# RWKV-7 inverse per pair of heads, diagonal state, and own tiles for the modulation weights

## The chip, the cores and the metric

The kernel runs on one core of a Trainium2 chip. The metric is the device time of one execution in microseconds (us), the median of the runs. TensorE (PE) multiplies matrices; a matmul loads its stationary operand (PEld in the profile) and streams the other. VectorE (DVE), ScalarE (ACT) and GpSimd (POOL) do the elementwise work, and all transfers here are issued on the queue of SyncE (SP).

## The reference

Two blocks run one after the other, all in fp32. The first has 512 tokens of width 1024, projects them with one matrix and feeds four mixers with four heads of 64 each; the second has two layers on 512 tokens and 256 of context. What matters here is the first block, and of the second the modulation that is computed from the conditioning vector alone.

```python
def rwkv7_time_mix(p, ...):            # one of the four mixers
    ...
    def step(state, inp):
        r_t, w_t, k_t, v_t, kk_t, a_t = inp
        sa = jnp.einsum('bhij,bhj->bhi', state, -kk_t)
        state = (state * w_t[:, :, None, :]
                 + sa[..., None] * (kk_t * a_t)[:, :, None, :]
                 + v_t[..., None] * k_t[:, :, None, :])
        return state, jnp.einsum('bhij,bhj->bhi', state, r_t)

def first_block(x, ...):
    h = rms_norm(x, norm_g[l])
    p = h @ w_in[l]
    (fq, fk, fv, fg, ff, sq, sk, sv, sg, rw, rg, lx, lg) = split_columns(p)
    y_fox = forgetting_attention(...)  # causal softmax with log forget gates
    y_sb = stick_breaking_attention(...)
    y_rw = rwkv7_time_mix(rw, ...)
    y_lru = rg_lru(lx, ...)
    y = jnp.concatenate([y_fox * silu(fg), y_sb * silu(sg), y_rw * silu(rg), y_lru * silu(lg)], -1)
    x = x + y @ w_out[l]
    ...
```

## The kernel before

**Layout.** Activations lie with the feature in the partitions: `x` and `y` are eight tiles of 128 features by 512 tokens. Matrices are multiplied at more than half precision by splitting: ScalarE writes the high part of a weight tile (`wh`, L149), VectorE the rest (`wl`, L150), and the same is done for the activations (`hH`, `hL`). Each product is then three matmuls, L178, L179 and L182 in the feature-major projection `proj_a`, or L202 to L204 in `proj_b`. A weight tile (`wtile`) is 128x1024 fp32, 512 KB, from a pool with three raw buffers `wr` and two each of `wh` and `wl`. It serves 24 matmuls of 512 columns.

**The order.** The program is written mixer by mixer in the order of `B_ORDER` (L41): `rw` RWKV, `sq` and `st` projection and core of stick-breaking attention, `fq` projection of fox (the forgetting attention), `lr` RG-LRU, `g4 g2 g6` three gate projections, `ad` the modulation of the first layer, `fo` the core of fox, `g0` its gate. A list scheduler then places each engine's instructions; a step that is written earlier has the higher priority, and a step whose inputs or buffers are late is passed by later ones. Each engine takes its list strictly in order. Buffers of the elementwise tiles come from lanes, with a count each (`B_LANES`); PSUM has three banks for `rw`, two for `at` (the attentions), one for `ad` and two for the projections.

**RWKV.** The 512 tokens are cut into four blocks of 128 (`b`), and the four heads into two pairs, each pair in the 128 partitions. `rwkv_gram` (L736) builds the products of the decayed operands inside each block (L762 multiplies one of them with v). `rwkv_inverse` (L765) inverts a unit triangular matrix for each block and head, by six levels of doubling: at each level GpSimd masks (L796), TensorE makes three products with 64x64 pieces (`prod`, L781), VectorE subtracts (L804, L805). `rwkv_free` (L821) multiplies the inverse with what needs no state (L828, L834). `rwkv_block` (L839) then walks the four blocks: u from the state (L848), the new state (L855, L856), the output (L866, L867, L869) and its copy by ScalarE (L870). The state of a pair is one 128x128 tile, of which a mask keeps the two diagonal quarters.

**Fox.** For each of four query tiles and four heads: scores (L534, with forget terms at L536 and L538), maximum (L540), exponential (L542), normalisation (L543, L544), transposes on TensorE (L397). After each second head follows the product with v (L521). The widths of the four query tiles are 128, 256, 384 and 512.

**The modulation.** `ada` (L954) runs over 12 groups. Of each it reads 2 MB of `wada` as four tiles of 512 KB in `wr` buffers, 48 in all, and multiplies 32 columns of the conditioning by it: 32 matmuls per group at L968, each two passes in the trace (384 matmuls, 768 passes). Then the row is copied, transposed (L397) and added to the bias in `mod` (L976).

**What follows.** `out_split` (L1169) projects `y` (L1185 to L1187). The residual additions are L439 and L444. The gate of a mixer is applied in `gates` (L481): ScalarE's activation (L486), VectorE's product (L488).

## Time and profile before

| | |
|---|---|
| median of 3 runs | 2241.99 us (2240.73 to 2243.96) |
| the profiled execution | 2235.85 us, span of its records 2234.1 us |
| mean granted clock of TensorE | 0.961 of 2.4 GHz |
| instructions | 31919 |
| busy: PE, PEld, DVE, ACT, POOL | 93%, 75%, 58%, 44%, 9% |
| chain of waits that ended last | PE 73%, DVE 13%, ACT 5%, DMA 5% |
| moved by DMA | 221.94 MB, mean 99 GB/s |

The busy share is of the whole span. The first phase, up to the first matmul of `out_split` at 440.6 us, is a fifth of it; the rest is that projection and the second block. PEclk in a window is the share of full clock that was granted, a mean over the stretch. A line of the waits gives an instruction group and what ended its waiting; a line of a group gives its shapes (partitions x elements), the count, busy time, the mean of one in ns, and the idle time of its engine ahead of it.

### The profile page before, as it was taken

Reading aid. Unit: us, or ns where it says so; the run is one execution under the profiler, and the core shown is the slowest. Engines: PE = TensorE matmul, PEld = TensorE weight load, DVE = VectorE, ACT = ScalarE, POOL = GpSimd, SP = SyncE. Lnnn points to the kernel's source line nnn. Section 1 sums busy time; section 2 is a strip of 40 time slices with the busy share of each in tenths; the row PEclk is TensorE's granted clock in tenths of the full one; section 3 lists DMA queues with packets and bytes.
Section 4 is the critical chain, followed back from the end, with each engine's and each line's share of the span. In section 5 each row is a group of like instructions: output and inputs, shape, how many; then the busy total and the mean of one; then the engine's idle time right before and its main releaser. Section 6 shows DMA issues by size and latency. Waiting matters only on the chain.

```text
span 2234.1 us, 31919 instructions
## 1 busy us (share of the span) xinstructions
PE 2078.4 (93%) x12676; PEld 1683.9 (75%) x12676; DVE 1293.1 (58%) x2275; ACT 990.2 (44%) x1874; POOL 193.6 (9%) x150
## 2 busy tenths in 40 slices
PE   6998997787999989989999999989988998999999
PEld 5876784577885847778888888879957756787877
DVE  5554523277655566576987344677656656554554
ACT  5533622254556764453132232455656554332432
POOL 0012100004000100230000000053000001000000
PEclk9998999898999989999999999999998999999999
DMA  4210137543110213432675212244212222232232
GB/s 154 76 57 2 42 108 244 191 132 105 48 53 6 81 38 116 162 114 90 203 236 164 73 51 81 89 148 139 72 50 70 69 77 71 90 101 92 82 112 85
DMA packets 86853, 221.94 MB, mean 99 GB/s; under 512 B 12976, under 2 KB 23984, under 8 KB 86576
## 3 DMA queue, kind: packets, MB, share of 16 engines
q1 hardware_dynamic: 86704, 219.90, 30.3%
q8 instruction: 100, 1.64, 0.3%
q14 instruction: 49, 0.40, 0.1%
HBM read 212.53 MB, written 7.34 MB: 98 GB/s over the span
## 4 chain that ended last, share of the span: by engine, by line
PE 73%; DVE 13%; ACT 5%; DMA 5%; issue 2%; POOL 0%; SPq 0%; DVEq 0%; ACTq 0%
PE ps L178 14%; PE ps L179 14%; PE ps L182 14%; PE ps L203 3%; PE ps L204 3%; PE ps L202 3%; DVE wl L150 2%; DMA wr<-in_wadaT 2%; PE ps L1448 2%; PE ps L1185 2%; PE ps L1186 2%; PE ps L1187 2%; DMA wr<-in_wada 2%; PE ps L521 1%; PE ps L397 1%
## 5 line engine op out<-in xcount | busy, mean ns | idle before, releaser
L178 PE MATMUL ps<-hH,wh 128*128 128x512 f32 (+1 forms) x1424 | 511.1, 364 | 20.2 <-ACT wh L149 13.0
L179 PE MATMUL ps<-hL,wh 128*128 128x512 f32 (+1 forms) x1424 | 501.9, 362 | 1.6 <-DVE hL L150 0.9
L149 ACT CAST wh<-wr 128x1024 fp32r<-128x1024 f32 (+4 forms) x302 | 284.1, 943 | 458.6 <-PE ps L179 378.5
L150 DVE TENSOR_TENSOR wl<-wr,wh 128x1024 fp32r<-128x1024 f32 (+4 forms) x266 | 288.6, 1087 | 253.4 <-ACT wh L149 244.9
L182 PE MATMUL ps<-hH,wl 128*128 128x512 f32 (+1 forms) x1248 | 432.4, 371 | 1.8 <-DVE wl L150 1.6
L178 PEld LDWEIGHTS ps<-hH,wh 128*128 128x128 f32 x1424 | 272.5, 192 | 73.6 <-ACT wh L149 14.8
L179 PEld LDWEIGHTS ps<-hL,wh 128*128 128x128 f32 x1424 | 272.4, 191 | 44.5 <-issue 1.8
L182 PEld LDWEIGHTS ps<-hH,wl 128*128 128x128 f32 x1248 | 223.5, 190 | 37.9 <-DVE wl L150 4.5
L203 PE MATMUL ps<-wl,hH 128*128 128x256 f32 x704 | 204.2, 291 | 12.6 <-DVE wl L150 12.5
L202 PE MATMUL ps<-wh,hH 128*128 128x256 f32 x704 | 204.4, 292 | 0.3 <-ACT wh L149 0.3
L204 PE MATMUL ps<-wh,hL 128*128 128x256 f32 x704 | 202.2, 290 | 0.0
L178 PE MATMUL ps<-uH,wh 128*128 128x512 f32 (+1 forms) x528 | 188.1, 362 | 7.0 <-ACT uH L149 4.1
L179 PE MATMUL ps<-uL,wh 128*128 128x512 f32 (+1 forms) x528 | 181.9, 358 | 0.2 <-DVE uL L150 0.2
L182 PE MATMUL ps<-uH,wl 128*128 128x512 f32 (+1 forms) x488 | 155.4, 365 | 2.5 <-DVE wl L150 2.4
L203 PEld LDWEIGHTS ps<-wl,hH 128*128 128x128 f32 x704 | 138.5, 197 | 16.2 <-DVE wl L150 14.6
L202 PEld LDWEIGHTS ps<-wh,hH 128*128 128x128 f32 x704 | 137.7, 196 | 4.0 <-issue 2.6
L204 PEld LDWEIGHTS ps<-wh,hL 128*128 128x128 f32 x704 | 137.8, 197 | 0.8 <-issue 0.3
L150 POOL TENSOR_TENSOR wl<-wr,wh 128x1024 fp32r<-128x1024 f32 (+1 forms) x36 | 84.1, 2343 | 603.8 <-ACT wh L149 584.4
L1691 DVE SCALAR_TENSOR_TENSOR xy<-ps,mod,xy 128x512 f32<-128x512 f32 (+1 forms) x96 | 60.8, 659 | 127.6 <-PE ps L182 124.5
L178 PEld LDWEIGHTS ps<-uH,wh 128*128 128x128 f32 x528 | 99.6, 189 | 34.2 <-ACT wh L149 8.4
L145 ACT COPY t<-ps 128x512 f32<-128x512 f32 (+4 forms) x131 | 64.3, 496 | 121.0 <-PE ps L397 70.6
L179 PEld LDWEIGHTS ps<-uL,wh 128*128 128x128 f32 x528 | 100.0, 189 | 15.9 <-DVE uL L150 0.7
(359 smaller groups left out, 3272.5 us busy)
## 6 DMA issues: line engine op xcount, KB each, us to landing
wr<-in_up SPq DMA_DIRECT2D x110, 512.0 KB, 3.6
wr<-in_wada SPq DMA_DIRECT2D x48, 512.0 KB, 4.4
wr<-in_wadaT SPq DMA_DIRECT2D x48, 512.0 KB, 4.3
wr<-in_win2b SPq DMA_DIRECT2D x36, 512.0 KB, 3.6
wr<-in_win SPq DMA_DIRECT2D x30, 512.0 KB, 3.6
wr<-in_dn SPq DMA_DIRECT2D x40, 320.0 KB, 2.9
wr<-in_dn SPq DMA_DIRECT2D x32, 384.0 KB, 3.2
wr<-in_wout SPq DMA_DIRECT2D x12, 512.0 KB, 3.7
```

Source lines behind the costliest of these rows:

```text
L145: self.nc.any.tensor_copy(out, in_)
L149: self.nc.scalar.copy(hi, src)
L150: (eng or self.nc.vector).tensor_tensor(lo, src, hi.bitcast(F32), ALU.subtract)
L178: nc.tensor.matmul(acc[s], wh, fh(k), start=(q == 0), stop=False)
L179: nc.tensor.matmul(acc[s], wh, fl(k), start=False, stop=False)
L182: nc.tensor.matmul(acc[s], wl, fh(k), start=False, stop=(q == nk - 1))
L202: nc.tensor.matmul(bank[:, i], fh(k), wh, start=start, stop=False)
L203: nc.tensor.matmul(bank[:, i], fh(k), wl, start=False, stop=False)
L204: nc.tensor.matmul(bank[:, i], fl(k), wh, start=False, stop=stop)
L1185: nc.tensor.matmul(acc, wh, yH[:, k], start=(q == 0), stop=False)
L1186: nc.tensor.matmul(acc, wh, yL[:, k], start=False, stop=False)
L1691: nc.vector.scalar_tensor_tensor(s.x[:, d, :], acc, self.mcol(5, d, s), s.x[:, d, :], ALU.mult, ALU.add)
```

## The change

Two parts of the program are written anew. The rest is the same text.

**RWKV.** The two heads of a pair share their tiles in the inverse, so that a level is one set of eight 64-column pieces instead of two of four. The products of the keys with v, inside the block for the output (`yk`) and for the state (`kv`), are made in `rwkv_gram` for all blocks at once, and `kv` is multiplied by the decay `fac` there. The state tiles are cleared once by GpSimd, and a block writes only the two 64x64 diagonal quarters; its output is VectorE's addition of `yk` instead of ScalarE's copy.

**The modulation.** `ada` reads tiles of 128x512, 256 KB, one for each of the eight row blocks of a group, 96 in all, into four buffers of their own (`wa`). The RWKV lane has 20 buffers instead of 29.

```diff
-B_LANES = dict(rw=29, at=4, qkv=5)
+B_LANES = dict(rw=20, at=4, qkv=5, wa=4)
...
-            zp = self.ps([P, 4, 64], "rw")
-            for b in range(4):
-                nc.tensor.matmul(zp[:, b], ga[:, b], tk("v", h, b), start=True, stop=True)
-            nc.scalar.copy(z[:, :, h], zp)
+            zp = self.ps([P, 2, 4, 64], "rw")
+            for e, m in enumerate((ga, gk)):
+                for b in range(4):
+                    nc.tensor.matmul(zp[:, e, b], m[:, b], tk("v", h, b), start=True, stop=True)
+            nc.scalar.copy(z[:, :, h], zp[:, 0])
+            nc.scalar.copy(yk[:, :, h], zp[:, 1])
+        kv = self.work.tile([P, 3, 64], F32, name=self.nm("kv"), tag="kv", bufs=2)
+        kp = self.ps([P, 3, 64], "rw")
+        for b in range(3):
+            for h in range(2):
+                nc.tensor.matmul(kp[h * 64 : h * 64 + 64, b], tk("ka", h, b), tk("v", h, b), start=True, stop=True)
+        nc.vector.tensor_tensor(kv, kp, d["fac"][:, 0:3]..., ALU.mult)
...
         for l in range(6):
-            for gb, up, cuh, clh, gd in heads:
-                an, xx = (t[:, i] for t in (two(),) for i in range(2))
-                nc.gpsimd.tensor_tensor(an, gd, c4(lmask[:, l : l + 1]), ALU.mult)
+            for d in pairs:
+                cu, cl = d["cu"], d["cl"]
+                an = t8()
+                nc.gpsimd.tensor_tensor(an, d["gd"], c8(lmask[:, l : l + 1]), ALU.mult)
...
-                tx = prod(cuh, lambda q, b: xx[q, b])
-                px = prod(xx, lambda q, b: cuh[q, b])
-                nc.vector.tensor_tensor(clh, clh, tx, ALU.subtract)
-                nc.vector.tensor_tensor(cuh, cuh, px, ALU.subtract)
+                tx = prod(cu, lambda q, u: xx[q, u])
+                px = prod(xx, lambda q, u: cu[q, u])
+                nc.vector.tensor_tensor(cl, cl, tx, ALU.subtract)
+                nc.vector.tensor_tensor(cu, cu, px, ALU.subtract)
...
+        d["sn"] = [self.work.tile([P, P], F32, name=self.nm("sn"), tag="sn", bufs=6) for _ in range(3)]
+        for sn in d["sn"]:
+            nc.gpsimd.memset(sn, 0.0)
...
-            sp = self.ps([P, P], "rw")
-            nc.tensor.matmul(sp, tok["be"][:, s], u, start=True, stop=False)
-            nc.tensor.matmul(sp, tok["ka"][:, s], tok["v"][:, s], start=False, stop=True)
...
-                nc.vector.tensor_tensor(sn, st, sp, ALU.add)
-                nc.vector.scalar_tensor_tensor(sn, sn, fac[:, b : b + 1], self.hsum, ALU.mult, ALU.mult)
+            base, f = kv[:, b], fac[:, b : b + 1]
+            if st is not None:
+                base = work.tile([P, 64], F32, name=self.nm("sb"), tag="sb", bufs=2)
+                for q in halves:
+                    nc.vector.scalar_tensor_tensor(base[q], st[q, q], f[q], kv[q, b], ALU.mult, ALU.add)
+            sp = self.ps([P, 64], "rw")
+            for h, q in enumerate(halves):
+                nc.tensor.matmul(sp[q], tk("be", h, b), u[:, h], start=True, stop=True)
+            sn = d["sn"][b]
+            for q in halves:
+                nc.vector.scalar_tensor_tensor(sn[q, q], sp[q], f[q], base[q], ALU.mult, ALU.add)
...
-            nc.tensor.matmul(yp[:, h], d["gk"][h][:, b], tk("v", h, b), start=(h == 0), stop=False)
-            nc.tensor.matmul(yp[:, h], d["gb"][h][:, b, 1, :], u[:, h], start=False, stop=(h == 1 and st is None))
+            nc.tensor.matmul(yp[:, h], d["gb"][:, 4 * h + b, 1, :], u[:, h], start=(h == 0),
+                             stop=(h == 1 and st is None))
...
-        nc.scalar.copy(y4[:, b], yp)
+        nc.vector.tensor_tensor(y4[:, b], yp, d["yk"][:, b], ALU.add)
...
-            for k0 in range(0, KT, 2):
-                w = self.wtile("wr")
-                self.dma(w.rearrange("p (k c) -> p k c", k=2), a["wada"][g, k0 : k0 + 2].rearrange("k p c -> p k c"))
-                for i in range(2):
-                    k = k0 + i
-                    for j in range(4):
-                        nc.tensor.matmul(acc[32 * j : 32 * j + 32, :], self.sc[:, k, :],
-                                         w[:, i * 512 + j * P : i * 512 + (j + 1) * P],
-                                         start=(k == 0), stop=(k == KT - 1))
+            for k in range(KT):
+                w = self.work.tile([P, 512], F32, name=self.nm("wa"), tag="wa", bufs=self.lanes["wa"])
+                self.dma(w, a["wada"][g, k])
+                for j in range(4):
+                    nc.tensor.matmul(acc[32 * j : 32 * j + 32, :], self.sc[:, k, :], w[:, j * P : (j + 1) * P],
+                                     start=(k == 0), stop=(k == KT - 1))
```

**What moves.** The scheduler places the instructions of the first phase in another order. In the new program the matmul of `ada` is at L979, and those of `rwkv_free` are at L836 and L842, of `rwkv_block` at L872 (state) and L879 (output), of `out_split` at L1195 to L1197.

SP's queue before, where the tiles of `wada` (`wr` from `in_wada`) follow the last tiles of the first block's projection weights (`in_win1`):

```order
L138 DMA wr509_2722<-in_win1 128x1024
L138 DMA wr512_2728<-in_win1 128x1024
L138 DMA wr519_2790<-in_win1 128x1024
L138 DMA wr522_2796<-in_win1 128x1024
L138 DMA wr532_2862<-in_wada 128x2x512
L138 DMA wr533_2872<-in_wada 128x2x512
L138 DMA wr534_2882<-in_wada 128x2x512
L138 DMA t2736_3838<-in_xT 128x512
```

After, in the first half of the block's projections:

```order
L138 DMA wr63_378<-in_win1 128x1024
L138 DMA wa513_2880<-in_wada 128x512
L138 DMA wa514_2886<-in_wada 128x512
L138 DMA wa515_2892<-in_wada 128x512
L138 DMA wr70_440<-in_win1 128x1024
L138 DMA wa516_2898<-in_wada 128x512
L138 DMA wr73_446<-in_win1 128x1024
L138 DMA wa520_2910<-in_wada 128x512
L138 DMA wr302_1712<-in_win1 128x1024
L138 DMA wa521_2916<-in_wada 128x512
L138 DMA wr305_1718<-in_win1 128x1024
```

The tiles of `wada` now stand between those of the projections, from the block's start on.

TensorE before, from the last product of fox (L521) over the last groups of `ada` (L968, row transposes L397) to the gate projection `g0` (L178, with `hH`), behind which the output projection L1185 comes:

```order
L521 MATMUL ps719_3726<-t2718_3724,t2451_2303 64x128
L397 MATMUL ps600_3318<-ident_131,row599_3316 128x128
L968 MATMUL ps601_3321<-wr602_3322,sc_96 32x128 x8
L968 MATMUL ps601_3321<-wr603_3332,sc_96 32x128 x8
...
L397 MATMUL ps607_3364<-ident_131,row606_3362 128x128
L968 MATMUL ps608_3367<-wr609_3368,sc_96 32x128 x8
...
L397 MATMUL ps614_3410<-ident_131,row613_3408 128x128
L178 MATMUL ps726_3748<-hH13_148,wh721_3737 128x512
```

After, within fox's seventh pair of heads, and at the end of the phase:

```order
L397 MATMUL ps705_3666<-ident_131,t2704_3662 128x128 x3
L521 MATMUL ps707_3672<-t2700_3653,t2416_2242 64x128
L979 MATMUL ps618_3395<-wa625_3432,sc_96 32x128 x4
L979 MATMUL ps618_3395<-wa626_3438,sc_96 32x128 x4
L521 MATMUL ps707_3672<-t2706_3670,t2416_2242 64x128
...
L521 MATMUL ps733_3762<-t2732_3760,t2417_2243 64x128
L1195 MATMUL ps749_3861<-hH744_3845,wh747_3856 128x512
```

The last `ada` matmuls stand inside fox's chain, the gate projection is ahead of them, and the output projection follows fox directly.

TensorE before, the first steps of RWKV's blocks (L855, L856 state; L866, L867 output), which stand behind the last gate projection:

```order
L855 MATMUL ps284_1604<-t2275_1567,t2100_575 128x128
L856 MATMUL ps284_1604<-t2104_589,t2102_582 128x128
L968 MATMUL ps531_2861<-wr532_2862,sc_96 32x128 x5
L968 MATMUL ps531_2861<-wr533_2872,sc_96 32x128 x3
L866 MATMUL ps286_1609<-t2104_589,t2132_676 128x64
L867 MATMUL ps286_1609<-t2275_1567,gb130_674 128x64
```

After, the same steps (L872 state, L879 output) behind the last of `rwkv_free` (L842):

```order
L842 MATMUL ps246_1534<-up175_832,t2123_651 64x128 x8
L872 MATMUL ps252_1552<-t2237_1503,t2100_575 64x64 x2
L178 MATMUL ps457_2546<-hH13_148,wh447_2493 128x512
L179 MATMUL ps457_2546<-hL14_149,wh447_2493 128x512
L182 MATMUL ps457_2546<-hH13_148,wl448_2494 128x512
...
L178 MATMUL ps457_2546<-hH13_148,wh447_2493 128x512
L879 MATMUL ps253_1557<-t2237_1503,gb130_674 128x64 x2
L179 MATMUL ps457_2546<-hL14_149,wh447_2493 128x512
```

They stand between the matmuls of a gate projection (L178, L179, L182).

## Rows read from the trace of the kernel before

**Rows 1.** The page, part 1: busy us, share of span, instructions.

```profile
PE 2078.4 (93%) x12676; PEld 1683.9 (75%) x12676; DVE 1293.1 (58%) x2275; ACT 990.2 (44%) x1874; POOL 193.6 (9%) x150
```

**Rows 2.** Windows: stretch, length, busy (PE, PEld, DVE, ACT, POOL), clock, DMA share, GB/s.

```profile
22.50:150.00 127.50, 124.18 (x581) 97.71 (x581) 69.11 (x105) 65.49 (x99) 13.86 (x14) 1.00 0.22 73
150.00:205.00 55.00, 48.08 (x419) 34.47 (x419) 23.91 (x45) 13.70 (x36) 10.36 (x17) 0.84 0.03 11
205.00:309.30 104.30, 101.30 (x1197) 79.91 (x1193) 45.12 (x81) 51.24 (x88) 13.89 (x22) 0.98 0.14 47
...
341.50:410.00 68.50, 53.45 (x651) 31.68 (x650) 20.05 (x60) 18.40 (x52) 2.66 (x1) 0.88 0.74 244
410.00:425.50 15.50, 7.43 (x130) 4.22 (x131) 0.62 (x5) 1.58 (x3) 0.00 (x0) 0.71 0.83 273
```

**Rows 3.** Waits of PE, 326 to 425 us: total us, times, longest us.

```profile
PE ps L968 <- DMA wr<-in_wada: 13.4, 16, 2.0
PE ps L397 <- ACT row L145: 3.0, 6, 0.7
PE ps L968 <- DVE mod L976: 2.2, 5, 0.7
```

**Rows 4.** Timeline of PE, g0 and the projection: start, us, work, idle before.

```profile
431.94 0.39 PE L182 MATMUL ps<-hH,wl 128*128 128x512 f32 x1
...
438.75 0.39 PE L182 MATMUL ps<-hH,wl 128*128 128x512 f32 x1
...
440.62 0.73 PE L1185 MATMUL ps<-hH,wh 128*128 128x512 f32 x2 [1.48 <-ACT hH L149]
```

**Rows 5.** Timeline of PE in the heads of fox.

```profile
343.08 0.70 PE L534 MATMUL ps<-t,xy 64*128 64x256 f32 x2
...
346.45 0.70 PE L534 MATMUL ps<-t,xy 64*128 64x256 f32 x2
...
369.31 0.91 PE L534 MATMUL ps<-t,xy 64*128 64x384 f32 x2
...
373.15 0.91 PE L534 MATMUL ps<-t,xy 64*128 64x384 f32 x2
...
400.61 1.12 PE L534 MATMUL ps<-t,xy 64*128 64x512 f32 x2
...
404.64 0.63 PE L397 MATMUL ps<-ident,t 128*128 128x128 f32 x4 [0.67 <-DVE t L544]
...
407.51 1.97 PE L521 MATMUL ps<-t,t 128*64 128x128 f32 x14
```

**Rows 6.** Timeline of PE: ada, gram, free.

```profile
329.59 1.50 PE L968 MATMUL ps<-wr,sc 128*32 128x128 f32 x42
...
173.01 1.06 PE L762 MATMUL ps<-t,t 128*128 128x64 f32 x8
...
310.32 2.00 PE L828 MATMUL ps<-t,t 128*128 128x64 f32 x16
...
317.19 0.49 PE L855 MATMUL ps<-t,t 128*128 128x128 f32 x2
```

**Rows 7.** Groups by line, 0 to 700 us: busy, mean ns, idle before.

```profile
L804 DVE TENSOR_TENSOR t<-t,ps 128x256 f32<-128x256 f32 x20 | 8.3, 413 | 15.8 <-PE ps L781 15.7
L488 DVE TENSOR_TENSOR xy<-xy,t 128x512 f32<-128x512 f32 x8 | 5.5, 688 | 11.6 <-ACT t L486 11.6
L796 POOL TENSOR_TENSOR t<-t,masks 128x256 f32<-128x256 f32 x24 | 19.0, 799 | 71.8 <-PE ps L781 65.7 <-ACT t L565 2.9 <-PE ps L762 2.5
```

**Rows 8.** DMA issues: KB each, median us from issue to landing.

```profile
wr<-in_win SPq DMA_DIRECT2D x30, 512.0 KB, 3.6
t<-in_lruw SPq DMA_DIRECT2D x1, 256.0 KB, 2.5
```

**Rows 9.** Waits of PE, 438 to 503 us; VectorE's timeline there.

```profile
PE ps L1185 <- DVE xy L439: 6.2, 2, 3.7
440.81 4.90 DVE L150 TENSOR_TENSOR hL<-xy,hH 128x512 fp32r<-128x512 f32 x8
```

More of the change, by code (lines that the diff above doesn't have):

```diff
@@ L771, in rwkv_inverse @@
-        c4 = lambda x: x.to_broadcast([P, 4, 64])
-        t4 = lambda t: t.rearrange("p (b t) -> p b t", b=4)
-        two = lambda: self.t2().rearrange("p (h b t) -> p h b t", h=2, b=4)
-        idc = c4(lmask[:, 6:7])
+        lo, hi = halves = (slice(0, 64), slice(64, 128))
+        c8 = lambda x: x.to_broadcast([P, 8, 64])
+        t8 = lambda: self.t2().rearrange("p (u t) -> p u t", u=8)
+        idc = c8(lmask[:, 6:7])
         def prod(lhs, rhs):
-            out = self.ps([P, 4, 64], "rw")
-            for b in range(4):
+            out = self.ps([P, 8, 64], "rw")
+            for u in range(8):
@@ L780, in prod @@
                 for q in halves:
-                    nc.tensor.matmul(out[q, b], lhs[q, b], rhs(q, b), start=True, stop=True)
+                    nc.tensor.matmul(out[q, u], lhs[q, u], rhs(q, u), start=True, stop=True)
             return out
-        heads = []
         for d in pairs:
-            cu, cl, gd = two(), two(), two()
-            d["up"] = [t4(self.t2()) for _ in range(2)]
-            for h in range(2):
-                nc.gpsimd.memset(d["up"][h][64:128, :, 0:64], 0.0)
-                for q in halves:
-                    nc.gpsimd.tensor_copy(gd[q, h], d["gb"][h][q, :, 0, q])
-                heads.append((d["gb"][h], d["up"][h], cu[:, h], cl[:, h], gd[:, h]))
+            d["cu"], d["cl"], d["gd"] = t8(), t8(), t8()
@@ L803, in rwkv_inverse @@
-                px = prod(xx, lambda q, b: cuh[q, b])
-                nc.vector.tensor_tensor(clh, clh, tx, ALU.subtract)
-                nc.vector.tensor_tensor(cuh, cuh, px, ALU.subtract)
-        lo, hi = halves
-        for gb, up, cuh, clh, _ in heads:
-            for q in halves:
-                nc.gpsimd.tensor_copy(up[q, :, q], cuh[q])
-            xp = self.ps([P, 4, 64], "rw")
-            for b in range(4):
-                nc.tensor.matmul(xp[hi, b], gb[lo, b, 0, hi], clh[lo, b], start=True, stop=True)
-            xx = two()[:, 0]
+                xx = t8()
@@ new lines, in rwkv_inverse @@
+                self.copy(xx, prod(an, lambda q, u: cl[q, u]))
+                tx = prod(cu, lambda q, u: xx[q, u])
+                px = prod(xx, lambda q, u: cu[q, u])
+                nc.vector.tensor_tensor(cl, cl, tx, ALU.subtract)
+                nc.vector.tensor_tensor(cu, cu, px, ALU.subtract)
+        for d in pairs:
+            cu, cl, gb, up = d["cu"], d["cl"], d["gb"], d["up"]
+            for q in halves:
+                nc.gpsimd.tensor_copy(up[q, :, q], cu[q])
+            xp = self.ps([P, 8, 64], "rw")
+            for u in range(8):
+                nc.tensor.matmul(xp[hi, u], gb[lo, u, 0, hi], cl[lo, u], start=True, stop=True)
+            xx = t8()
@@ L815, in rwkv_inverse @@
             self.copy(xx[hi], xp[hi])
-            px = self.ps([P, 4, 64], "rw")
-            for b in range(4):
-                nc.tensor.matmul(px[lo, b], xx[hi, b], cuh[hi, b], start=True, stop=True)
+            px = self.ps([P, 8, 64], "rw")
+            for u in range(8):
+                nc.tensor.matmul(px[lo, u], xx[hi, u], cu[hi, u], start=True, stop=True)
             nc.scalar.activation(up[lo, :, hi], px[lo], AF.Copy, scale=-1.0)
@@ L827, in rwkv_free @@
             for b in range(4):
-                nc.tensor.matmul(up0[:, b, h], up[h][:, b], z[:, b, h], start=True, stop=True)
+                nc.tensor.matmul(up0[:, b, h], up[:, 4 * h + b], z[:, b, h], start=True, stop=True)
         d["u0"] = self.t2().rearrange("p (b h i) -> p b h i", b=4, h=2)
```

34 lines of the change are left out of this document (17 added, 17 removed).

## The prediction

> **What bounds the kernel now.** I read the page first. TensorE (PE) is busy for 93% of the span [rows 1], and the instruction orders of the two programs differ, names apart, only up to the first output projection of the first block (the loop of out_split, L1185). So what has to be forecast is one number: how much earlier that projection starts. The first phase, where all edits lie, is then cut by stage [rows 2]. From 22.5 to 150 us and again from 205 to 309 us PE hardly idles: projections run back to back. The weak stretches are 150 to 205 us (6.9 us idle, granted clock 0.84, that is a mixture of the two levels 1.2 and 2.4 GHz), 341 to 410 us (15 us idle, 0.88) and 410 to 425 us (8 us idle, 0.71). In the last two DMA moves 244 to 273 GB/s, nearly all of it the modulation weights of ada.
>
> Why PE idles there is in its waits: between 326 and 425 us it stood 13.4 us for wr tiles of in_wada, and 5.2 us more for the row copies and the mod additions that end a group of ada [rows 3]. After 410 us there is nothing but ada, tile after tile at the pace of the transfers, and the gate projection g0 and the output projection (start 440.62 us) queue behind it on PE, g0 at 0.227 us a pass (30 passes from 431.94 to 438.75 us) [rows 4]. The attention of fox lies in the same stretch. It is a chain of its own: scores, softmax on VectorE and ScalarE, transposes, product. PE takes the heads one after the other, and each ada tile that has not landed pushes the next link back [rows 5]. So this stage is bound by two things at once, the bytes of ada and the chain of fox, since in_wada shares the three wr buffers with the projections' weights and stands behind all of them on SP's queue.
>
> **The change, part by part.**
>
> Ada. Its 96 tiles of 256 KB get four buffers of their own. The order shows what comes of that: 224 of the 384 ada matmuls now stand ahead of fox's second query tile, in 32 places (before, only three stand ahead of the end of the last gate projection), the first four tiles ahead of the first projection; 160 (40 tiles) stay in the tail. PE's price for a pass is 0.0357 us (42 passes in 1.50 us [rows 6]), and each matmul is two passes. Of the 224, 16 fall before the first projection, where PE waits for the norm anyway, and 73 stand among the steps of stick, between 175 and 212 us, where PE had 6.9 us of idle [rows 2]; these are free. The other 135 cost 135 x 2 x 0.0357 = 9.6 us of a PE that is full. The 73 fill 5.2 us of the idle in stick; if that cover were gone it would be 5.2 us more. The 1.7 us of idle that are left there I count as a gain, since ada's passes fill them with work that need not be done later.
>
> RWKV. In the inverse, pairs of products of 4x64 columns become one of 8x64: the same 480 matmuls, so PE gains nothing. VectorE: 40 subtractions of 0.41 us become 20 of about 0.69 us (the price of a 512-wide one), so 16.5 us become 13.8 (the other group of 20, L805, has the same mean); POOL: 24 of 0.80 us (19.0 us) become 12 of twice the width, at most the same 19.0 us, at least half [rows 7]. Both engines are half idle there and PE hardly waits for them, so I cost this at nothing; the cover is the stick and projection work that stands between the levels. Bounds: no gain below 0, and at most the 2.7 us of VectorE. The kappa products (12 matmuls for the state, 16 for y) move out of the steps into the gram. At 0.12 us a pass with a 128-row weight (8 passes in 1.06 us [rows 6]) they cost 28 x 2 x 0.12 = 6.7 us of full PE. The triangular products L828 and L834, 7.0 us from 310.3 to 317.2 us, and the block steps stood in the tail and now stand between the projections of the gates. The new steps hold 40 matmuls: 40 x 2 x 0.12 = 9.6 us. The chain of a step loses one VectorE addition and gains split halves; with projections between the links nobody waits for it. The six memsets of the states on POOL and the eight additions that replace ScalarE's copies of y run on engines with room. So RWKV adds 6.7 + 7.0 + 9.6 = 23.3 us ahead of the tail and takes its steps out of it.
>
> Start of the tail. The last gate projection ended at 309.3 us. Now: 309.3 + 9.6 + 23.3 - 1.7 = 340.5 us.
>
> The tail. Six pairs of heads remain (two of each width 256, 384, 512), and g0. Score to score within a pair takes 3.4 us at 256 columns and 3.8 at 384 (with ada between), and at 512 4.0 us to the transposes and 0.6 for these, 4.6 in all [rows 5]. For copy and product I add 1.2, 1.7 and 2.3 us (the 14 passes of the last took 1.97 us). So a pair is 2 x 3.4 + 1.2 = 8.0, 2 x 3.8 + 1.7 = 9.3, and 2 x 4.6 + 2.3 = 11.5 us; all six 57.6 us. g0, 48 matmuls at 0.227 us (10.9 us), stands between the first two heads, in which PE idles for an estimated half of the 3.4 us, 1.7 us each: 7.5 us more. The first pair thus ends at 340.5 + 8.0 + 7.5 = 356.0 us. The next three pairs (8.0 + 9.3 + 9.3 = 26.6 us) carry 32 of the tail's 40 tiles. Four are in the buffers; 28 tiles, 7.3 MB, at the 244 GB/s of this stage [rows 2] need 30.1 us. So the transfers are late by 3.5 us there. I add 1.4 us for the latency of a refill (256 KB landed in 2.5 us [rows 8], at 244 GB/s a tile comes every 1.1), and 2.4 us for the ends of the five groups (5.2 us in 11 waits, 0.47 us each [rows 3]): 7.3 us. The last two pairs (23.0 us) have no ada. End: 356.0 + 26.6 + 7.3 + 23.0 = 412.9 us, instead of 440.6: 27.7 us.
>
> Behind it. Rows 2, 3, 6, 7 of y are split for the output projection during fox now (the order has six of the eight subtractions early), where before all eight, 4.9 us of VectorE, stood at 440.8 us and made PE wait 6.2 us for L439, which was queued behind them [rows 9]. I take half of that wait, 3 us; the bounds are 0 and 6.2.
>
> SP's queue carries 48 issues more and is in order: a wa issue whose buffer is still held blocks the wr issues behind it. In the places where they alternate, wr is fetched one projection (24 passes, 5.4 us) ahead, so up to some 3 us of blocking cost nothing. The transfer itself: 512 KB landed in 3.6 us and 256 KB in 2.5 us [rows 8], so half the size costs 70% of the time, and 48 transfers more carry 48 x 1.4 = 67 us of latency in all. With four in flight and an empty queue that is hidden up to 309 us; in the tail it is in the 1.4 us. The Trainium skill (DMA: Bandwidth & Descriptors, section Bandwidth) speaks against this edit: transfers should be batched to 1 MiB or more, and its section on the anatomy of one DMA gives each a fixed cost of about 2.0 us. By that alone, with nothing hidden, the 48 added transfers would be 96 us, an estimate from the page, and the kernel slower; the rows have a smaller step, and whether it shows is the second rival below.
>
> Sum: 27.7 + 3.0 = 30.7 us off the profiled execution of 2235.85 us (span 2234.1), so 2205. The median of the runs is 2241.99, 6 us above that execution, and 30.7 us off it is 2211 us.
>
> **The rivals.** Larger gain: the waits in the tail vanish (7.3 us), the blocks fill idle PE and the tail starts 6 us sooner, and at a full granted clock the six pairs lose 5 us; with the 31 us that is 49 us: 2193 us. For it: the tail's stretches have 0.88 and 0.71 today [rows 2]. Against it: PE stays half idle there, as now.
>
> The transfers bind. With 1 MB in flight instead of 1.5 MB the rate falls to two thirds of 244, to 163 GB/s, and the 28 tiles take 45 us instead of 30: 15 us less gain, 2226 us. For it: the tail empties all four buffers within one head, so a refill cannot start early. Against it: the landing time falls with the size. This is where the rule of the Trainium skill (DMA: Bandwidth & Descriptors, section Bandwidth) would show.
>
> Given back: the output projection starts early but finds its weights late, as wout's tiles stand among ada's last tiles on SP. Losing 12 us there makes 2223 us. Against it: the first five are ahead of the last ada tile.
>
> Slower: the 32 places ahead of the tail stop a full PE, each until its tile lands, since PE is in order and SP's queue holds wa behind wr. A wait for in_wada was 0.84 us on average and 2.0 us at most [rows 3]. At 0.96 us each the gain is gone; at 1.3 us the sum is 42 us and the time 2253 us. Against it: up to 309 us DMA is busy for 22% or less [rows 2], and a tile has one projection's time to land.
>
> That the change doesn't do what it says can be excluded for the placement, which the order shows.
>
> **How the numbers follow.** Forecast 0.57 (its own range 2200 to 2219), larger gain 0.15, the transfers bind 0.13, given back 0.06, slower 0.05, and 0.04 for a sum near zero from several of these. The forecast and the first three rivals are all faster: 0.91. About 0.2% (4.5 us) is what a measurement can tell from no change; same 0.04, slower 0.05. The range 2190 to 2230 holds the forecast, most of the larger gain and both small gains, some 0.85; it reaches to the bounds of the hL term and of the transfer rate.
>
> **What would show it.** The first ada matmul before 22 us; the output projection's first matmul near 413 us; PE idle for in_wada's tiles in the tail a few us instead of 13.4, and under 5 us in all ahead of it; no stretch with ada alone; the inverse's products at the same sum of PE time. I am wrong if the last gate projection ends much later than 340 us (waits in the full stretch), if heads in the tail are further apart than 5 us (transfers), or if the time from the output projection's start to the end grows.

## The result, and the profile after

The changed kernel takes 2217.43 us (median of 4 runs, 2213.03 to 2220.95), the kernel before in the same comparison 2242.70 us. The ratio is 0.9887, interval 0.9868 to 0.9907: 25.3 us less. The forecast was 2211 us and faster; the range 2190 to 2230 us holds the time, and the gain is 5.4 us smaller than the 30.7 forecast.

In the profiled execution (2217.67 us, span 2215.9) TensorE is as full as it was [rows 1]:

```profile
PE 2075.2 (94%) x12700; PEld 1678.3 (76%) x12700; DVE 1296.4 (59%) x2267; ACT 991.5 (45%) x1864; POOL 185.5 (8%) x134
```

The windows of the changed kernel, columns as in [rows 2] and with cuts at its own landmarks, show where it went. The last gate projection but g0 ends at 334.1 us, the first of the remaining pairs of fox's heads at 352.3, the fourth at 389.5, and the output projection starts at 419.1:

```profile
22.50:150.00 127.50, 123.31 (x701) 93.52 (x701) 65.98 (x108) 63.82 (x99) 10.38 (x8) 1.00 0.36 120
150.00:205.00 55.00, 53.27 (x470) 39.21 (x470) 22.89 (x43) 15.37 (x41) 9.47 (x10) 1.00 0.19 58
205.00:309.30 104.30, 103.17 (x1555) 83.90 (x1555) 53.64 (x103) 51.28 (x87) 9.37 (x10) 1.00 0.28 87
309.30:334.10 24.80, 24.80 (x114) 19.84 (x112) 14.08 (x26) 13.06 (x19) 0.00 (x0) 1.00 0.24 73
334.10:352.30 18.20, 18.20 (x168) 13.63 (x167) 6.23 (x14) 7.56 (x16) 0.00 (x0) 1.00 0.59 195
352.30:389.50 37.20, 31.31 (x300) 16.93 (x299) 9.58 (x27) 9.52 (x28) 0.00 (x0) 0.72 0.61 205
389.50:419.10 29.60, 19.07 (x67) 9.54 (x66) 6.17 (x14) 7.95 (x17) 2.65 (x1) 0.58 0.00 1
```

From 150 to 205 us the idle 6.9 us are 1.7 now, and the granted clock is 1.00 instead of 0.84. From 205 us to the end of the gates PE is full. Then the clock falls: 0.72 over the next three pairs, 0.58 over the last two, the lower level (0.5 is 1.2 GHz) for most of it, with DMA idle. What PE waits for there (its waits from 326 to 425 us, in total us, times, longest us) is another thing than in [rows 3]:

```profile
PE ps L397 <- DVE t L544: 11.9, 7, 3.2
PE ps L979 <- DMA wa<-in_wada: 2.1, 6, 0.6
PE ps L397 <- ACT row L145: 1.8, 3, 0.9
```

The 13.4 us for in_wada are 2.1, and fox's own chain, VectorE's normalisation at L544, has come up as the wait, with 11.9 us.

The timeline of PE (start, duration, work, idle before): the end of the last gate projection, the first scores of three pairs, the scores, transposes and product of the last, and the output projection:

```profile
333.83 0.39 PE L182 MATMUL ps<-hH,wl 128*128 128x512 f32 x1
...
352.31 0.70 PE L534 MATMUL ps<-t,xy 64*128 64x256 f32 x2
...
389.51 1.12 PE L534 MATMUL ps<-t,xy 64*128 64x512 f32 x2
...
402.92 2.07 PE L534 MATMUL ps<-t,xy 64*128 64x512 f32 x2
...
415.35 1.09 PE L397 MATMUL ps<-ident,t 128*128 128x128 f32 x4 [3.15 <-DVE t L544]
...
416.37 2.77 PE L521 MATMUL ps<-t,t 128*64 128x128 f32 x16
...
419.08 0.80 PE L1195 MATMUL ps<-hH,wh 128*128 128x512 f32 x1
```

Two scores of 512 columns took 2.07 us here; in [rows 5] the same took 1.12. The projection starts 21.5 us sooner than in [rows 4]. From there to the end of the span it is 1796.8 us instead of 1793.5, so 18.2 us of the span are gained. That is 7.1 us less than the medians give: the profiled execution of the kernel before (2235.85 us) lies 6.9 us under the median of its runs, that of the changed kernel at its median. Where these 7 us lie, two profiles do not show.

### The profile page after: what moved, and what is told of

It is laid out like the page before. It is cut to its first block, busy times and chain, and to the rows that moved or that the text cites. A ratio compares the mean times of both kernels' runs of the same rounds, so it can differ in the third digit from the quotient of the medians.

```text
span 2215.9 us, 31987 instructions
## 1 busy us (share of the span) xinstructions
PE 2075.2 (94%) x12700; PEld 1678.3 (76%) x12700; DVE 1296.4 (59%) x2267; ACT 991.5 (45%) x1864; POOL 185.5 (8%) x134
## 4 chain that ended last, share of the span: by engine, by line
PE 75%; DVE 12%; ACT 6%; DMA 4%; issue 2%; POOL 0%; SPq 0%; POOLq 0%; DVEq 0%; ACTq 0%
PE ps L178 15%; PE ps L179 14%; PE ps L182 14%; PE ps L203 3%; PE ps L204 3%; PE ps L202 3%; DVE wl L150 2%; PE ps L1458 2%; DMA wr<-in_wadaT 2%; PE ps L1195 2%; PE ps L1196 2%; PE ps L1197 2%; PE ps L397 2%; PE ps L1449 1%; PE ps L790 1%
## 5 line engine op out<-in xcount | busy, mean ns | idle before, releaser
L178 PE MATMUL ps<-hH,wh 128*128 128x512 f32 (+1 forms) x1424 | 509.3, 363 | 16.5 <-ACT wh L149 13.0
L179 PE MATMUL ps<-hL,wh 128*128 128x512 f32 (+1 forms) x1424 | 499.4, 361 | 1.5 <-DVE hL L150 0.8
L182 PE MATMUL ps<-hH,wl 128*128 128x512 f32 (+1 forms) x1248 | 431.2, 370 | 4.7 <-DVE wl L150 4.6
L150 DVE TENSOR_TENSOR wl<-wr,wh 128x1024 fp32r<-128x1024 f32 (+4 forms) x266 | 289.3, 1090 | 247.2 <-ACT wh L149 237.0
L178 PEld LDWEIGHTS ps<-hH,wh 128*128 128x128 f32 x1424 | 270.3, 190 | 70.6 <-ACT wh L149 14.7
L179 PEld LDWEIGHTS ps<-hL,wh 128*128 128x128 f32 x1424 | 270.3, 190 | 44.3 <-issue 2.8
L182 PEld LDWEIGHTS ps<-hH,wl 128*128 128x128 f32 x1248 | 222.8, 189 | 41.3 <-DVE wl L150 7.6
L203 PE MATMUL ps<-wl,hH 128*128 128x256 f32 x704 | 204.8, 292 | 12.7 <-DVE wl L150 12.6
L178 PE MATMUL ps<-uH,wh 128*128 128x512 f32 (+1 forms) x528 | 188.3, 363 | 6.5 <-ACT uH L149 3.7
L179 PE MATMUL ps<-uL,wh 128*128 128x512 f32 (+1 forms) x528 | 182.2, 358 | 0.2 <-DVE uL L150 0.2
L182 PE MATMUL ps<-uH,wl 128*128 128x512 f32 (+1 forms) x488 | 155.4, 365 | 1.8 <-DVE wl L150 1.8
L178 PEld LDWEIGHTS ps<-uH,wh 128*128 128x128 f32 x528 | 99.7, 189 | 33.9 <-ACT wh L149 8.4
L179 PEld LDWEIGHTS ps<-uL,wh 128*128 128x128 f32 x528 | 100.1, 190 | 15.8 <-DVE uL L150 0.7
```

Source lines behind the costliest of these rows:

```text
L150: (eng or self.nc.vector).tensor_tensor(lo, src, hi.bitcast(F32), ALU.subtract)
L178: nc.tensor.matmul(acc[s], wh, fh(k), start=(q == 0), stop=False)
L179: nc.tensor.matmul(acc[s], wh, fl(k), start=False, stop=False)
L182: nc.tensor.matmul(acc[s], wl, fh(k), start=False, stop=(q == nk - 1))
L203: nc.tensor.matmul(bank[:, i], fh(k), wl, start=False, stop=False)
```

## The experiments

Each ratio is to runs of the kernel before on the same chip, with its 95% interval. "Start" is the output projection's first matmul in the profiled execution, "rest" the span behind it.

| kernel | median us | ratio to before | start us | rest us |
|---|---|---|---|---|
| before | 2242.70 | | 440.6 | 1793.5 |
| changed | 2217.43 | 0.9887 (0.9868 to 0.9907) | 419.1 | 1796.8 |
| e1 ada's own tiles alone | 2213.56 | 0.9877 (0.9840 to 0.9914) | 414.0 | 1799.8 |
| e2 RWKV alone | 2237.98 | 0.9993 (0.9971 to 1.0015) | 443.9 | 1799.7 |
| e3 changed, 512 KB tiles | 2210.46 | 0.9880 (0.9840 to 0.9920) | 426.2 | 1779.4 |
| e4 changed, extra work | 2202.48 | 0.9841 (0.9803 to 0.9879) | 414.9 | 1787.2 |
| e5 changed once more | 2216.27 | 0.9909 (0.9885 to 0.9932) | 415.4 | 1796.6 |
| e6 changed, g0 late | 2203.13 | 0.9852 (0.9825 to 0.9879) | 426.3 | 1782.5 |
| e7 changed, fox in RWKV's banks | 2176.97 | 0.9735 (0.9703 to 0.9767) | 395.8 | 1784.0 |
| e8 e7 and g0 late | 2192.00 | 0.9812 (0.9781 to 0.9842) | 402.7 | 1785.4 |
| e9 e7, six wa buffers | 2180.27 | 0.9730 (0.9690 to 0.9770) | 396.1 | 1781.2 |
| e10 before, fox in RWKV's banks | 2231.42 | 0.9955 (0.9934 to 0.9975) | 449.9 | 1779.7 |
| e11 e1, fox in RWKV's banks | 2240.12 | 0.9993 (0.9971 to 1.0014) | 452.6 | 1780.6 |

The table has to be read by its last two columns. The rest of the program computes the same everywhere, yet it takes from 1779 to 1800 us. The scheduler plans the whole program with simulated times, so an edit in the first phase changes its choices later on: behind the start, the traces have 31 of TensorE's some 9290 matmuls in another place in the changed kernel than before, in e1 to e4 and e6 to e11 476 to 1191. When these lists are laid side by side, the difference lies in one stretch: between 300 and 480 us behind the start e3, e4, e6, e7, e9, e10 and e11 gain 12 to 17 us on the kernel before, the changed kernel (both profiles) and e2 at most 2, e8 4 and e1 7. Which choice there is worth it was not tried. Start and rest are of one execution each, and the executions of one kernel lie up to 18 us apart (e2: 2229.96 to 2248.13 us, with 2245.39 the profiled one). So a theory on the first phase is judged by the start, and a median only together with the rest.

**Once more the same (e5).**

> The changed kernel itself once more, beside the next ones. The first runs of one and the same kernel lay 8 us apart, and the stretch from the output projection's start to the end, the same instructions in the same order, took between 1779 and 1800 us. Expected: projection start within 3 us of 419.1, the rest between 1779 and 1800, and a median of 2210 to 2220 us.

The start, from the timeline:

```profile
415.36 0.80 PE L1195 MATMUL ps<-hH,wh 128*128 128x512 f32 x1
```

It lies 3.7 us before that of the first profile, a little outside the expected 3; the rest is the same to 0.2 us. A start is thus known to about 4 us, and the gain in the start is 21.5 to 25.3 us.

**Ada's tiles alone (e1) and RWKV alone (e2).** e1 is the kernel before with the new reads of ada:

```diff
-B_LANES = dict(rw=29, at=4, qkv=5)
+B_LANES = dict(rw=25, at=4, qkv=5, wa=4)
...
-            for k0 in range(0, KT, 2):
-                w = self.wtile("wr")
...
+            for k in range(KT):
+                w = self.work.tile([P, 512], F32, name=self.nm("wa"), tag="wa", bufs=self.lanes["wa"])
+                self.dma(w, a["wada"][g, k])
```

> The kernel before with ada's own tiles alone (four of 256 KB); RWKV is the old code, with 25 lane buffers instead of 29. Theory 1, the gain is the bytes of ada that leave the tail: most of the 25 us is here, 2219 to 2226 us, ada's passes lie in the stick stretch and its granted clock is near 1.00 instead of 0.84. Rival, the gain is RWKV's shorter program: 2236 to 2245 us.

The windows of e1, stick stretch, columns as above:

```profile
150.00:205.00 55.00, 52.22 (x446) 36.08 (x449) 22.60 (x46) 13.87 (x37) 6.91 (x13) 1.00 0.30 96
```

and the projection's first matmul (timeline):

```profile
414.01 0.50 PE L1182 MATMUL ps<-hH,wh 128*128 128x512 f32 x1 [0.82 <-ACT t L486]
```

e2 is the changed kernel with that edit undone.

> The changed RWKV with ada as before, in the 512 KB wr tiles. Theory 1: the tail is still bound by ada's transfers, so 2232 to 2242 us, the output projection starts no earlier than 432 us, PE waits over 10 us for in_wada in the tail and the clock of the stick stretch stays near 0.84. Rival, the RWKV change alone shortens the phase: 2217 to 2226 us.

Its waits of PE from 300 to 445 us:

```profile
PE ps L981 <- DMA wr<-in_wada: 18.9, 17, 2.8
```

the stick stretch in the windows, and the projection's first matmul:

```profile
150.00:205.00 55.00, 49.87 (x492) 38.30 (x492) 22.07 (x37) 12.93 (x33) 10.61 (x11) 0.91 0.03 11
```

```profile
443.94 0.73 PE L1198 MATMUL ps<-hH,wh 128*128 128x512 f32 x2 [1.49 <-ACT hH L149]
```

The start comes forward by 26.6 us in e1, whose median is even better than expected, and goes back by 3.3 in e2, less than the 4 us to which a start is known. Ada's own tiles are the whole gain of the changed kernel, and RWKV's new form by itself gains nothing: PE still waits for in_wada at the end, 18.9 us in e2. The stick stretch tells the same of the clock: 1.00 with ada's passes in it, 0.91 without them in e2, 0.84 in [rows 2]. In e1 RWKV's steps, in the old form, still stand in the tail, between the heads of fox. That e2's clock lies between the two while it has no ada there, since the kappa products (L763, L770) fill a part, is argued, not shown.

**The size of a transfer (e3).** Ada's tiles are 512 KB again, but two buffers of their own hold them:

```diff
-                w = self.wtile("wr")
+                w = self.work.tile([P, 1024], F32, name=self.nm("wa"), tag="wa", bufs=self.lanes["wa"])
...
+B_LANES = dict(rw=20, at=4, qkv=5, wa=2)
```

(against the old ada, in the changed kernel).

> The changed kernel with ada's own tiles at 512 KB, two buffers, so the same memory and half as many transfers. If the size of a transfer costs (a half-size tile takes 70% of the time to land), this one is faster than the changed kernel by 3 to 8 us: 2210 to 2214. If four small buffers are what lets a tile come early, it is slower by 3 to 8 us: 2221 to 2226. Theory 1 (the tail is a chain of heads, transfers are nearly hidden): within 4 us of 2217.

Its transfers (KB each, us to landing):

```profile
wa<-in_wada SPq DMA_DIRECT2D x48, 512.0 KB, 4.3
```

its waits from 326 to 430 us, and the projection's first matmul:

```profile
PE ps L981 <- DMA wa<-in_wada: 8.1, 6, 4.1
```

```profile
426.16 0.52 PE L1198 MATMUL ps<-hH,wh 128*128 128x512 f32 x1
```

The median falls to where the first line of the expectation had it, and that line is still wrong: the start is 7 to 11 us later than in the two profiles of the changed kernel, and the rest 17 us shorter. The larger tile makes PE wait longer, 8.1 us instead of 2.1, up to 4.1 at once. For the start the four small tiles are better, as the second line had it ("four small buffers are what lets a tile come early"). Whether it is their size or their number is not shown, since e3 changes both.

**Extra work in the last pairs (e4).** Behind the scores of each of the last four heads stand eight more matmuls, whose sum goes nowhere:

```diff
-                nc.tensor.matmul(z[:, qt * P : nk], self.identb, self.caus[:, 0, :], start=False, stop=True)
+                mk = nc.tensor.matmul(z[:, qt * P : nk], self.identb, self.caus[:, 0, :], start=False, stop=True).ins
+                if qt == 3:
+                    with self.tc.issue_after(mk):
+                        fl = self.ps([P, 512], "ad")
+                        for q in range(8):
+                            nc.tensor.matmul(fl, self.hx[0](q)[:, 0:P], self.hx[0](q), start=(q == 0), stop=(q == 7))
```

> The changed kernel with eight extra 512-wide matmuls (1.8 us at full clock) behind the scores of each of the last four heads of fox, whose results nobody uses. Theory 2, the last two pairs take 29.6 us instead of the 23.0 of the prediction since TensorE, with no ada left to do, falls to a granted clock of 0.59: with the extra work the clock is near 1.00, the two pairs take 22 to 25 us, the output projection starts at 412 to 415 us, and the kernel is 4 to 7 us faster than the changed one, though it does more. Rival, the pairs are slow by VectorE's and ScalarE's steps: the pairs take 29 to 37 us, and the time is the same or up to 7 us longer.

The window of the last two pairs in e4, columns as above:

```profile
388.90:414.90 26.00, 20.27 (x115) 12.13 (x113) 9.89 (x19) 11.16 (x24) 2.66 (x1) 1.00 0.01 4
```

and of its timeline, scores and extra matmuls of the third of these heads, and the projection:

```profile
401.12 1.12 PE L534 MATMUL ps<-t,xy 64*128 64x512 f32 x2
...
402.56 2.09 PE L543 MATMUL ps<-hH 128*128 128x512 f32 x8
...
414.94 0.79 PE L1200 MATMUL ps<-hH,wh 128*128 128x512 f32 x1 [0.82 <-ACT t L486]
```

With 8.4 us more to do (four groups of 2.1 us) the two pairs take 26.0 us instead of 29.6, at a granted clock of 1.00 instead of 0.58, and the scores are back at 1.12 us. That is the direction theory 2 expected, and it speaks against the rival, by which the pairs had to take 29 to 37 us. The size is smaller: 26.0 and not 22 to 25. And part of it is scatter, as the same two pairs show in e5, the changed kernel once more. In e1 RWKV's steps fill them, and they are shorter still (windows of e5, then of e1):

```profile
387.90:415.40 27.50, 16.96 (x67) 9.09 (x66) 6.19 (x14) 7.97 (x17) 2.65 (x1) 0.67 0.00 1
```

```profile
389.20:414.00 24.80, 22.10 (x153) 16.09 (x152) 10.61 (x30) 9.40 (x23) 0.00 (x0) 1.00 0.00 1
```

The four profiles stand in one order: 29.6 us at a clock of 0.58, 27.5 at 0.67, 26.0 and 24.8 at 1.00. By these the clock costs the changed kernel 1.5 to 4.8 us in the two pairs. Of the 13.8 us between the profiled executions of the changed kernel and e4, 9.7 are in the rest.

**Real work in the last pairs (e6).** If extra work helps, g0's 48 matmuls might do it:

```diff
+                if step == "g0":
+                    with self.tc.issue_after(self.fmark):
+                        steps[step]()
```

(`fmark` is the last score matmul of the first head of fox's fourth query tile).

> The changed kernel, where the gate projection g0 (48 matmuls, 10.9 us) may start on TensorE only behind the first scores of fox's last query tile; it then stands in the last two pairs. Theory 2 (TensorE falls to half clock there since it has too little to do): the pairs keep nearly the full clock and take 25 to 30 us with g0 in them, the heads ahead lose at least 7 us, the projection starts at 406 to 413 us, and the kernel is 5 to 12 us faster than the changed one. Rival, g0 only moves: start 417 to 424 us, the time within 3 us.

The windows of e6, where g0 stood before and now doesn't:

```profile
341.50:380.00 38.50, 34.30 (x309) 17.72 (x309) 8.02 (x27) 8.13 (x26) 0.00 (x0) 0.69 0.68 225
```

and the projection:

```profile
426.31 0.79 PE L1201 MATMUL ps<-hH,wh 128*128 128x512 f32 x1
```

Both expectations fall: the start is 426.3 us, later than in the changed kernel. The last two pairs begin only 3.2 us sooner (scores at 386.30 instead of 389.51 us), much less than the 10.9 us that g0 is long, with the clock at 0.69 from 341.5 to 380 us, where the changed kernel has 0.83; and they take 40.0 us with g0 in them instead of 29.6. Work moved from one half-idle stretch to another moves the low clock with it. The median is better by the rest alone (1782.5).

**Fox in RWKV's banks (e7).** All of the above takes the chain of the heads as given. Scores, transposes and products of fox share two PSUM banks (tag "at"), and RWKV's three are free in the tail of the changed kernel:

```diff
-                pts.append(self.flip(p, qt + 1, "at"))
+                bk = "rw" if qt else "at"
+                pts.append(self.flip(p, qt + 1, bk))
                 if h % 2:
                     self.pv_pair(pts[h - 1 :], [v(i) for i in range(qt + 1)], h // 2,
-                                 self.y[:, h // 2, qt * P : (qt + 1) * P])
+                                 self.y[:, h // 2, qt * P : (qt + 1) * P], tag=bk)
```

> The changed kernel, where fox's transposes and products of query tiles two to four use the three PSUM banks of RWKV, idle by then, instead of the two banks that hold the scores. Theory 3 (the tail is one head after the other, since scores, transposes and product share two banks): heads overlap, the bytes of ada bind instead (40 tiles at 244 GB/s are 43 us from 334 us on), the projection starts at 380 to 395 us, and the kernel is 20 to 35 us faster than the changed one. Rival, the steps of VectorE and ScalarE bind: start 410 to 420 us, the time within 6 us.

The windows of e7, columns as above, for the first four pairs and the last two:

```profile
334.30:370.20 35.90, 33.84 (x320) 21.00 (x319) 14.36 (x34) 14.60 (x37) 0.00 (x0) 1.00 0.64 206
370.20:395.80 25.60, 20.39 (x215) 11.56 (x214) 7.04 (x19) 9.90 (x24) 2.65 (x1) 0.93 0.48 147
```

its timeline, scores of two heads and the projection:

```profile
380.26 1.12 PE L534 MATMUL ps<-t,xy 64*128 64x512 f32 x2
...
383.77 1.12 PE L534 MATMUL ps<-t,xy 64*128 64x512 f32 x2
...
395.77 0.50 PE L1196 MATMUL ps<-hH,wh 128*128 128x512 f32 x1
```

its waits from 330 to 396 us:

```profile
PE ps L980 <- DMA wa<-in_wada: 3.5, 10, 1.0
PE ps L397 <- DVE t L544: 1.9, 1, 1.9
```

The start is 395.8 us, 19.6 to 23.3 us ahead of the changed kernel's, and just behind the 380 to 395 expected. In the last pair a head's scores follow the previous ones by 3.5 us, where those of the changed kernel came 6.3 us apart (402.92 and 409.27 us), the clock stays near full without any extra work, and the wait for L544 falls from 11.9 to 1.9 us. Most of the gain is not in the last two pairs: these take 25.6 us instead of 29.6, the first four, with g0, 35.9 instead of 55.4. So the tail of the changed kernel was bound by its two banks, and the low clock was mostly a consequence of that. With 2177 us this is, with e9, the fastest kernel here: 0.9735 of before. Of the 39 us by which its median lies below the changed kernel's (20 to 35 were expected), the profiles show 20 to 23 in the start and 13 in the rest.

**What binds then (e8, e9).** e8 holds g0 back in e7, behind the first scores of the third query tile.

> e7 with g0 held behind the first scores of fox's third query tile. Theories 2 and 3 together: the tail's start has less to do and its end more, so the projection starts 2 to 8 us ahead of e7's. Rival, ada's bytes bind the tail in both: start within 2 us of e7's.

Start 402.7 us, 7 later than e7: a miss for both theories, and the same lesson as e6. e9 gives ada six buffers in e7 and RWKV 18, in the same memory.

> e7 with six wa buffers and 18 RWKV buffers in the same memory. If ada's bytes bind e7's tail (its PE waited 3.5 us for in_wada there and the last ada matmul stood 7 us ahead of the output projection), more tiles leave the tail: projection start 385 to 393 us instead of 395.8. If the heads bind: start within 3 us of e7's.

The last ada matmuls start at 368.7 us instead of 388.9, and the start is the same: with the banks free it is the heads again that set the end, not the bytes of ada.

**Do the banks help without the change (e10, e11)?** e10 is the kernel before, e11 is e1, both with the edit of e7.

> The kernel before with the three RWKV banks for fox's transposes and products, nothing else. Theory 1 (in the kernel before ada's 48 transfers of the tail bind first, the chain of heads second): start of the projection within 8 us of 440.6 and a median of 2225 to 2245 us. Rival, the two banks bound the kernel before as well: start at 415 to 428 us.

Waits of PE in e10 from 300 to 445 us:

```profile
PE ps L969 <- DMA wr<-in_wada: 17.6, 18, 2.8
```

and the projection:

```profile
449.92 0.73 PE L1186 MATMUL ps<-hH,wh 128*128 128x512 f32 x2 [1.49 <-ACT hH L149]
```

The start is 9 us later than before, a little more than the 8 expected, and not earlier as the rival had it: ada's bytes did bind the old tail, with 17.6 us of waiting. The median is 10 us better by the rest alone.

> The kernel before with ada's own tiles and fox's transposes and products in RWKV's banks, RWKV in the old form. If RWKV's new form is worth nothing in itself: start within 5 us of e7's 395.8. If the steps of the old form, which still stand in the tail and hold these banks, delay fox: start at 402 to 414 us.

The timeline of e11: RWKV's last step (L870), the next scores of fox (L534), the projection:

```profile
386.91 0.44 PE L870 MATMUL ps<-sn,ar 128*128 128x128 f32 x2
...
401.54 1.22 PE L534 MATMUL ps<-t,xy 64*128 64x256 f32 x2 [1.17 <-ACT t L542]
...
452.59 0.79 PE L1183 MATMUL ps<-hH,wh 128*128 128x512 f32 x1
```

Both lines of the expectation are far too early. RWKV's old form still stands in the tail there, its steps, which use the three banks, run to 387 us, and fox, which now needs them too, goes on only at 401.5 us: the start is 452.6. So RWKV's new form, worth nothing in e2, is what lets RWKV end before the tail, and e7 stands on both parts of the change.

## Why the prediction was right, point by point

**The number.** The range holds the time, but by the profiled executions the forecast was 2205 us and 2217.67 were measured, 12.5 us more: the start is 6.2 us later than forecast, and the rest 3.3 us longer instead of 3.0 shorter. The medians are only 6.4 us apart from the forecast because the execution on which it was built lay 6.1 us under the median known then, while that of the changed kernel lies at its median. That part is luck.

**Its own signs.** Of the three signs of being wrong, two came up: heads further apart than 5 us (5.7, 6.4 and 6.3 us within three of the last five pairs), and a rest that grows. The first was put down to transfers in advance; it was mostly the heads' own chain and the clock. Of the signs of being right, one did not: the inverse's products were to keep their PE time, and they fell from 37.8 to 32.7 us (lines below).

**One number decides.** Right in the main. The time between the output projection's start and the end differs by 3.3 us in the profiles and 3.1 in e5. That the two orders differ only up to that projection is not quite so: by the traces they also differ at its beginning and some 373 and 1090 us behind it.

**Ada ahead of the tail.** Right, as the waits show: 2.1 us for in_wada in the tail against "a few us instead of 13.4", and e1 shows it to be the source of the gain.

**Start of the tail, forecast 340.5 us, measured 334.1.** The sum was 309.3 + 38.1 (the passes added: 9.6, 5.2 and 23.3) - 6.9. By the windows PE's busy time from 22.5 us to the tail grew from 273.6 to 304.6 us, by 31.0, and its idle time fell from 13.2 to 7.1, by 6.2: 309.3 + 31.0 - 6.2 = 334.1. The idle time was sized right. The passes that came in cost what was priced, 37.9 us in all if each instant is counted once, though only in the sum: ada 18.2 instead of 14.8, RWKV's 19.8 instead of 23.3 (its price of 0.12 us a pass is a little under its own row, 1.06 us for 8, and the new passes took less still). The work grew 7 us less, since other work got shorter. Groups of PE ahead of the tail (busy us, mean ns | idle before), before:

```profile
L781 PE MATMUL ps<-t,t 64*64 64x64 f32 x960 | 33.6, 225 | 2.0 <-DVE sm L543 1.3 <-ACT t L145 0.6
...
L559 PE MATMUL ps<-t,xy 64*128 64x128 f32 (+3 forms) x32 | 14.6, 539 | 0.0
...
L781 PE MATMUL ps<-ident,t 64*64 64x64 f32 x64 | 4.2, 316 | 0.0
```

and after, where L790 is the same product:

```profile
L790 PE MATMUL ps<-t,t 64*64 64x64 f32 x960 | 30.4, 219 | 0.0
...
L559 PE MATMUL ps<-t,xy 64*128 64x128 f32 (+3 forms) x32 | 12.8, 482 | 0.0
...
L790 PE MATMUL ps<-ident,t 64*64 64x64 f32 x64 | 2.3, 221 | 0.0
```

The three groups fell from 52.4 to 45.5 us, 6.9 less. There are two causes. The prediction filled the idle time of the stick stretch and counted the 1.7 us that were left, but not that the granted clock, 0.84 there, would come back to 1.00 for everything else in it: stick's scores (L559) take 12.8 us in e1 as well. The inverse's products are another matter. In e1, which has the old form, 784 of the 960 passes stand ahead of 345 us, where the clock was 1.00 throughout (groups of PE, 0 to 345 us):

```profile
L781 PE MATMUL ps<-t,t 64*64 64x64 f32 x784 | 30.0, 222 | 0.0
```

They take as long as all 960 of the new form, 38 ns a pass instead of 32 (35 instead of 32 if each instant is counted once). So their part of the fall is not the clock but goes with the new form, and "the same 480 matmuls, so PE gains nothing" was wrong; why they got cheaper was not tried.

**The inverse.** Right in what it costs the other engines: VectorE's subtraction takes 0.68 us as priced, and GpSimd's mask 1.17 us, so 14.0 us for the 12 where the bounds were half and the whole of 19.0. By groups, 0 to 700 us, beside [rows 7]:

```profile
L803 POOL TENSOR_TENSOR t<-t,masks 128x512 f32<-128x512 f32 x12 | 14.0, 1168 | 42.1 <-PE ps L790 37.7 <-PE ps L763 4.1 <-issue 0.2
...
L812 DVE TENSOR_TENSOR t<-t,ps 128x512 f32<-128x512 f32 x10 | 6.8, 683 | 7.3 <-PE ps L790 7.3
```

That it would bring the start nothing by itself was right too, as e2 shows; that it would bring PE nothing was not (above).

**The tail, forecast 72.4 us, measured 85.0.** This is the term that was mis-sized. First pair with g0: 18.2 instead of 15.5 us; next three: 37.2 instead of 33.9; last two: 29.6 instead of 23.0. The 4.6 us from one head's scores to the next held for the first of the last four heads, still at the full clock (389.51 to 394.10 us); the three behind it took 8.8, 6.3 and 9.8 us, where 6.9, 4.6 and 6.9 were priced. Of a pair of 512 columns the prediction said 11.5 us, from [rows 5]; these rows come from heads between which ada's passes ran. It moved the passes away and kept the durations. Without them PE waits 2.3 to 3.2 us per head for L544, the clock falls, and each step of the chain that runs on PE lengthens: 2.07 us for scores instead of 1.12, 2.77 for the product of 16 passes. The prediction had seen half of it: against its first rival it set that PE stays half idle, and made of that no gain, where it was a loss. e4 and e1, in which the clock stays up, still took 26.0 and 24.8 us, so 2 to 3 us of the 6.6 remain without the low clock; how much of them the work that stands between the heads there costs is not shown. What e7 adds is the reason for the waits: a chain in two banks, which the prediction took as given.

**The transfers.** The landing of a 256 KB tile was taken as 2.5 us, from one lone transfer. It was longer (KB, us; the tiles of 512 KB before, then those of the changed kernel):

```profile
wr<-in_wada SPq DMA_DIRECT2D x48, 512.0 KB, 4.4
```

```profile
wa<-in_wada SPq DMA_DIRECT2D x96, 256.0 KB, 3.5
```

so the half-size tile costs 0.8 of the 4.4 us of the old one, not 0.7. It did not matter to the sum: the rival "the transfers bind" would have shown as waiting for in_wada, 15 us of it; there were 2.1. The Trainium skill (DMA: Bandwidth & Descriptors, section Bandwidth) asks for transfers of 1 MiB and more. That is a rule on bandwidth. Here the tiles of 256 KB brought the start forward and those of 512 KB in e3 less so. The fixed cost that the prediction quotes from the same page is given there for transfers that GpSimd issues; here SyncE issues them, and no run measures it apart.

**Behind the start.** The forecast was 3.0 us for VectorE's earlier splits. The wait for L439 fell by 1.7 us, from the 6.2 in [rows 9] (waits from 419 to 482 us):

```profile
PE ps L1195 <- DVE xy L439: 4.5, 2, 3.7
```

Sixteen us behind the start the changed kernel is 1.8 us ahead of the old one, 56 us behind it 0.6. At 1050 us it is 1.4 us ahead, at 1100 us 1.5 behind, and between the two lies the last place where the orders differ; the code is unchanged there.

**Sum.** Start of the tail 6.4 us better, the tail 12.6 worse: 419.1 instead of 412.9. Two errors partly cancelled, which is luck; the clock and what fills TensorE have a part in both. The mechanism, ada's bytes leaving the tail, was right; what then bound the tail is the chain of the heads, which the prediction had priced too low.

## What to carry to other kernels

Where TensorE waits on a chain, look at which buffers or PSUM banks make the chain serial before looking for work to fill its gaps: the two banks of fox were worth about as much as the whole change. Here work that was taken out of a half-idle stretch took the clock with it (e6: 0.69 instead of 0.83), and what was put into one brought it back (e4), so durations read between other work do not hold without that work. A rewrite that moves nothing by itself can be what makes the next edit possible (e7 against e11), and with a scheduler that plans the whole program a median alone says little of an edit; compare landmarks.

## What the runs showed of the hardware

The granted clock followed what TensorE had to do in the stretch: 0.58 in the last two pairs of the changed kernel (0.67 once more in e5), 1.00 in the same pairs with 8.4 us of useless matmuls, which made them 1.5 to 3.6 us shorter. The same stick stretch had 0.84 in the kernel before, 0.75 in e10, 0.91 in e2, and with ada's passes in it 1.00 in the changed kernel and its variants and in e1, but 0.94 in e11.
